# Gate and up projections on Trainium2: one of seven block products computed by seven products of quarter blocks

## The chip, the core and the metric

The kernel runs on one core of one Trainium2 chip. The metric is the device time of one execution in microseconds (us), the median over runs. A core has five engines with a queue of instructions each, worked in order: TensorE (PE in the profile, its weight loads PEld), VectorE (DVE), ScalarE (ACT), GpSimd (POOL) and SyncE (SP), which here issues DMAs. Operands lie in SBUF (128 partitions); TensorE writes its sums to PSUM, eight banks of 128 x 512 f32.

## What is computed

One post-norm encoder layer on 1024 tokens of width 1024: an input projection, bidirectional retention and windowed attention, an output projection, a layer norm that gives h, then a feed-forward part with a small gated embedding and a second layer norm. The part that matters here:

```python
g = jnp.einsum('bsd,df->bsf', h, w_ffn_gate)
up = jnp.einsum('bsd,df->bsf', h, w_ffn_up)
ffn = jnp.einsum('bsf,fd->bsd', jax.nn.silu(g) * up, w_ffn_down)
```

D = 1024, the hidden width is 2816 = 22 tiles of 128 ("f tiles").

## The kernel before

All large products are done in split precision: `split` (L70) puts a rounded high half on ScalarE (`hi`, L71) and the remainder on VectorE (`lo = raw - hi`, L72; both inputs in SBUF), and `mm3c` (L781) issues three matmuls, hi x hi, hi x lo and lo x hi, on L783, L784 and L785, into one PSUM bank. Each is 128 x 128 weights by 512 columns.

The gate and up stage takes two f tiles at a time (a `Pair`, 11 in all) and sees each pair as a product of 2 x 2 blocks: the left matrix is the weight (rows: the two f tiles; columns: the two halves of D), the right one h transposed (halves of D by halves of the tokens). It uses Winograd's form of Strassen's scheme: seven block products instead of eight, with sums of blocks before and after. Product 1 is a11 b11, product 2 a12 b21, products 5, 6, 7, 3 and 4 use sums. With M1 the first product: u2 = M1 + M6, u3 = u2 + M7 (the code adds M7 onto M6's bank and then M1), c11 = M1 + M2, c22 = u3 + M5, c21 = u3 + M4, c12 = u2 + M5 + M3. Products that share a sum accumulate in one bank: 1 and 2 in bank X, 6, 7 and 4 in Y, 5 and 3 in Z. Before a later product is added onto a bank, the value that it holds must have been read.

The right operands (h and its sums, `RIGHT`, L1160) are split once and stay in SBUF. The work is a list of units (`gunits`, L1290): one product p for m = 0 (gate) or m = 1 (up), 12 matmuls each; below "unit p/m". The order in a pair is 1, 6, 5, 2, 7, 4, 3 (pair 0: 1, 2, 6, 5, 7, 4, 3). A unit has three parts:

- `prep`: the weights are loaded by SP into `raw` and `ln` (`load`, L1176; at unit 1/m of the pair); the split of the unit's left operand into an operand slot, in turn from four `w` and four `u` tiles (L1197); behind unit 1/m GpSimd makes four block sums of weights (`s_sums`, L1183; L1187, L1188, L1190, L1191).
- `mm`: the matmuls (L1201).
- `post` (L1223): reads of the bank. `add` (L1231) is a VectorE addition of a bank and an SBUF tile (L1232); the copy of product 1 is on ScalarE (L1238). `finish` (L1211) applies Silu to the gate on ScalarE (L1215) and multiplies it with up on GpSimd (L1217). `asum` (L1219) makes sums of finished blocks for the down projection on GpSimd (L1221). Results go to DRAM (`ad`) by SP, two units later.

The order of the work is written out by hand: every engine executes its instructions in the order in which the program issues them. The loop at L1616 issues for each unit k its matmuls, its `post`, and then `ahead(2, k + 1 + min(8, 4 + k))` (L1583), which issues preparations up to eight units ahead; then stores that are due:

```python
for k in range(NG):
    gunits[k][1]()
    gunits[k][2]()
    ahead(2, k + 1 + min(8, 4 + k))
    while stores and stores[0][0] <= k:
        stores.pop(0)[1]()
```

Evicted blocks lie in `ev` tiles from a ring of eight (`pair_tile`, L1164); a pair takes seven. Each pair takes three of four bank tags in turn, two banks each (L1205). After this stage the down projection runs with its own lists (`d_units`, `d_step`).

Of the kernel before, what the change touches and what calls it, by code (L numbers as in the profile page):

```python
# [9 lines left out]
F32 = mybir.dt.float32  # L10
F32R = mybir.dt.float32r
AF = mybir.ActivationFunctionType
ALU = mybir.AluOpType
# [3 lines left out]
P = 128  # L17
# [4 lines left out]
HF = 512  # L22
# [20 lines left out]
def layer(tc, xT, xn, w_first, w_mt, w_rv, w_out, w_pg, w_pe, pT, w_gu, w_dn,  # L43
          consts, dec_b, dec_c, sink, gng, lnp, out):
    nc = tc.nc
    act, dve, pool, pe, sp = nc.scalar, nc.vector, nc.gpsimd, nc.tensor, nc.sync
# [8 lines left out]
    wp = cstack.enter_context(tc.tile_pool(name="wp", bufs=4))  # L55
# [14 lines left out]
    def split(raw, hi, lo):  # L70
        act.activation(hi, raw, AF.Copy)  # L71
        dve.tensor_tensor(lo, raw, hi.bitcast(F32), ALU.subtract)  # L72
# [77 lines left out]
    with tc.manual_schedule(engines={mybir.EngineType.DVE, mybir.EngineType.SP}):  # L150
        for kt in range(KT):
# [26 lines left out]
            w = wf[kt % 2]  # L178
# [10 lines left out]
    cst = cp.tile([P, C_W], F32, name="cst")  # L189
# [530 lines left out]
    with tc.manual_schedule(engines={mybir.EngineType.PE}):  # L720
# [7 lines left out]
        a = Attention(0, ytile(1))  # L728
# [11 lines left out]
        Q, X = (lambda q: (r.scores, q)), (lambda q: (r.turn, q))  # L740
        Y, E = (lambda q: (r.out, q)), (lambda q: (r.evict, q))
# [3 lines left out]
        for i in range(1, NPAIR):  # L745
# [26 lines left out]
    def ct(shape, tag, bufs=None, dt=F32):  # L772
        return cpool.tile(list(shape), dt, tag=tag, bufs=bufs, name=nm(tag))
# [7 lines left out]
    def mm3c(o, lh, ll, rh, rl, start, stop):  # L781

        pe.matmul(o, lh, rh, start=start, stop=False, skip_group_check=True)  # L783
        pe.matmul(o, lh, rl, start=False, stop=False, skip_group_check=True)  # L784
        pe.matmul(o, ll, rh, start=False, stop=stop, skip_group_check=True)  # L785
# [169 lines left out]
    c11 = [r[:, i * HF:(i + 1) * HF] for r in (rawt(2 * HF), rawt(2 * HF)) for i in range(2)]  # L955
# [5 lines left out]
    Z = four("b")  # L961
# [9 lines left out]
    X = four("a")  # L971
# [121 lines left out]
    X = four("a")  # L1093
# [25 lines left out]
    for k in range(4):  # L1119
        c = slice(k * P, (k + 1) * P)  # L1120
# [11 lines left out]
    Z = four("b")  # L1132
# [28 lines left out]
    sarena = arena8  # L1161
    ptags = ("mm", "s", "t", "o")

    def pair_tile():  # L1164
        return a_tile([P, 2, HF], "ev")

    stores = []

    class Pair:
# [23 lines left out]
        def prep(self, p, m, k):  # L1193
            src = {1: lambda: self.raw[m, 0, 0], 2: lambda: self.raw[m, 0, 1], 4: lambda: self.raw[m, 1, 1],
                   5: lambda: self.s[m][1], 6: lambda: self.s[m][0], 7: lambda: self.s[m][2],
                   3: lambda: self.s[m][3]}[p]()
            t = wp.tile([P, 2, HF], F32R, tag="w", bufs=4, name=nm("w")) if k % 2 == 0 else ct([P, 2, HF], "u", 4, F32R)  # L1197
            split(src, t[:, 0, :], t[:, 1, :])
            self.ops[p, m] = t

        def mm(self, p, m):  # L1201
            g = {1: 0, 2: 0, 6: 1, 7: 1, 4: 1, 5: 2, 3: 2}[p]
            first = p in (1, 6, 5)
            if first:
                self.bank[g, m] = bank(ptags[(3 * self.n + g) % 4])  # L1205
            b, w, r = self.bank[g, m], self.ops[p, m], RIGHT[p]
            for kt in range(4):
                c = slice(kt * P, (kt + 1) * P)
                mm3c(b, w[:, 0, c], w[:, 1, c], r[:, 0, kt, :], r[:, 1, kt, :], first and kt == 0, kt == 3)

        def finish(self, name, m):  # L1211

# [10 lines left out]
        def post(self, p, m, k):  # L1223
            ev, X, Y, Z = self.ev, self.bank.get((0, m)), self.bank.get((1, m)), self.bank.get((2, m))

            def get(name):
                if m == 0:
                    ev[name] = pair_tile()
                return ev[name][:, m, :]

            def add(name, left, right):  # L1231
                dve.tensor_tensor(get(name), ev[left][:, m, :], right, ALU.add)  # L1232

            a = lambda name: ev[name][:, 1, :]
            s = lambda name: ev[name][:, 0, :]
            wait = 2 if self.n < NP - 1 else 8
            if p == 1:
                act.activation(get("s1"), X, AF.Copy)  # L1238
            elif p == 6:
                add("u2", "s1", Y)  # L1240
            elif p == 2:
                c = get("c11")
                if m == 0:
                    act.activation(c, X, AF.Silu)
                else:
                    dve.tensor_tensor(c, ev["c11"][:, 0, :], X, ALU.mult)
            elif p == 7:
                add("u3", "s1", Y)
                add("c22", "u3", Z)
                self.finish("c22", m)  # L1250
            elif p == 4:
                add("c21", "s1", Y)
                self.finish("c21", m)
                if m:
                    self.asum("c21", a("c21"), a("c11"), ALU.subtract)
                    stores.append((k + wait, lambda: sp.dma_start(ad[self.n, 2, :, 0, :], s("c21"))))
                    self.asum("c11", s("c21"), a("c22"), ALU.subtract)
                    stores.append((k + wait, lambda: sp.dma_start(ad[self.n, 0], ev["c11"])))
                    self.asum("c22", a("c22"), a("c21"), ALU.subtract)
                    stores.append((k + wait, lambda: sp.dma_start(ad[self.n, 3], ev["c22"])))  # L1260
            elif p == 3:
                add("c12", "u2", Z)
                self.finish("c12", m)
                if m:
                    self.asum("c12", a("c12"), s("c11"), ALU.add)
                    stores.append((k + wait, lambda: sp.dma_start(ad[self.n, 1], ev["c12"])))

    NP = NHID // 2
    gunits = []
    pairs2 = [Pair(n) for n in range(NP)]  # L1270

    def g_unit(n, p, m, k):
        pr = pairs2[n]

        def prep():
            if p == 1 and n:
                pr.load(m)
            pr.prep(p, m, k)
            if p == 1:
                if n:  # L1280
                    pr.s_sums(m)
                else:
                    pr.s_sums(m, (0,))
                    if m:
                        pr.s_sums(0, (1,))
                        pr.s_sums(1, (1,))

        return prep, lambda: pr.mm(p, m), lambda: pr.post(p, m, k)
# [323 lines left out]

    ET = mybir.EngineType
    with tc.manual_schedule(engines={ET.PE, ET.DVE, ET.Activation, ET.Pool, ET.SP}):
        ahead(2, 4)
        for k in range(NG):  # L1616
            gunits[k][1]()
            gunits[k][2]()
            ahead(2, k + 1 + min(8, 4 + k))
            while stores and stores[0][0] <= k:  # L1620
                stores.pop(0)[1]()
            j = k + 1 - NG
            if j == -6:
                arenas_a()
                op_arena(ct([P, 4, 2, HF], "h0a", dt=F32R))
                op_arena(big16((P, 4, 2, HF)))
                op_arena(big16((P, 4, 2, HF)))
                arena("chain", ct([P, 8, HF], "h0b"), 8)
            if j == -4:
                op_arena(big16((P, 4, 2, HF)))  # L1630
                arena("b", big.tile([P, 8, HF], F32, tag="H", bufs=4, name=nm("H")), 8)
            if j >= -6:
                ahead(0, j + 7)
            if j >= -4:
                ahead(1, j + 5)
        arena("chain", ct([P, 8, HF], "h2"), 8)
        op_arena(ct([P, 4, 2, HF], "h3", dt=F32R), 4)
        rings["op"] += [ct([P, 2, HF], "u", 4, F32R) for _ in range(2)]
        for k in range(ND):
            d_step(k)  # L1640
# [85 lines left out]
```

## Time and profile before

| | us |
|---|---|
| median of 3 runs | 1181.1 (1179.52 to 1181.5) |
| the profiled execution | 1180.62 |
| its span, first to last instruction | 1178.8 |
| mean granted TensorE clock | 0.997 |
| gate and up stage on TensorE | 540 to 960 |
| GpSimd's block sums (L1187, L1188, L1190, L1191), 88 in all | 131.4 busy |

The profile's page gives busy time by engine, a picture of the span in 40 slices, the chain of work that ended last, and groups of instructions by line. Rows of the timeline read: start, duration (both us), engine, line, operation, output <- inputs, shape, count, and in brackets how long the engine sat idle before and what released it. A matmul's record (0.39 us for 512 columns) overlaps the next one's; the step between two starts is what one costs. In rows of stretches the columns are: stretch, length, busy us and number of instructions of PE, PEld, DVE, ACT and POOL, granted clock, share of the DMA engines, GB/s. In rows of waits: who <- on whom: us in total, times, longest.

### The profile page before, as it was taken

The page shows a single profiled execution, that of the slowest core. Times are in us where ns is not written, and L with a number is a line of the kernel's source. Part 1 is how long each engine was busy: PE and PEld are TensorE (multiplying, and loading weights), DVE is VectorE, ACT ScalarE, POOL GpSimd, SP SyncE. Part 2 cuts the span into 40 slices and gives each one's busy share as a digit, 9 for nine tenths or more (in the row PEclk, how much of TensorE's full clock was granted, in tenths as well). Part 3 has the DMA queues.
Part 4 walks back from the last instruction along what each step waited for, and adds up shares of the span by engine and source line. Part 5 has one row for each costly group of instructions (what it writes and reads, how often), then busy time and mean ns, then how long its engine had stood idle before and what let it go on. Part 6 is the DMA issues. An engine that isn't in the chain of part 4 may idle for free.

```text
span 1178.8 us, 17058 instructions
## 1 busy us (share of the span) xinstructions
PE 1167.3 (99%) x6068; PEld 968.4 (82%) x6068; DVE 767.3 (65%) x1310; ACT 534.4 (45%) x1049; POOL 365.5 (31%) x346
## 2 busy tenths in 40 slices
PE   9999999999999999999999999999999999999996
PEld 7888888888888888888788888888888888888885
DVE  5566678776849688948655455545555465774777
ACT  5566348777756265214332333323333325563463
POOL 2001010202010020004765647464655341134242
PEclk9999999999999999999999999999999999999998
DMA  6345656545346955665323331233213179999977
GB/s 253 107 148 215 241 182 240 188 152 205 123 151 240 361 186 195 242 221 176 124 76 120 134 110 70 90 134 135 77 63 129 72 221 323 354 270 229 258 164 208
DMA packets 80661, 211.71 MB, mean 180 GB/s; under 512 B 9536, under 2 KB 14784, under 8 KB 80576
## 3 DMA queue, kind: packets, MB, share of 16 engines
q1 hardware_dynamic: 71936, 193.84, 46.2%
q0 software_dynamic: 8640, 16.78, 8.0%
q8 instruction: 48, 0.79, 0.3%
q14 instruction: 37, 0.30, 0.1%
HBM read 139.29 MB, written 62.13 MB: 171 GB/s over the span
## 4 chain that ended last, share of the span: by engine, by line
PE 94%; DVE 3%; ACT 1%; issue 1%; DMA 1%; DVEq 0%; SPq 0%; ACTq 0%
PE bmm L77 6%; PE bs L785 6%; PE bs L783 6%; PE bs L784 6%; PE bmm L79 6%; PE bmm L78 6%; PE bt L783 5%; PE bt L785 5%; PE bt L784 5%; PE bmm L785 5%; PE bmm L783 5%; PE bmm L784 5%; PE bo L785 5%; PE bo L783 5%; PE bo L784 5%; PE bo L565 2%
## 5 line engine op out<-in xcount | busy, mean ns | idle before, releaser
L77 PE MATMUL bmm<-H,w 128*128 128x512 f32 x240 | 97.2, 405 | 0.2 <-ACT H L71 0.2
L79 PE MATMUL bmm<-H,w 128*128 128x512 f32 x240 | 94.1, 392 | 0.0
L78 PE MATMUL bmm<-H,w 128*128 128x512 f32 x240 | 94.0, 392 | 0.0
L1187 POOL TENSOR_TENSOR H<-ln 128x512 f32<-128x512 f32 x22 | 28.9, 1312 | 180.2 <-ACT w L71 96.1
L1217 POOL TENSOR_TENSOR ev<-ev 128x512 f32<-128x512 f32 x33 | 55.4, 1679 | 90.6 <-DVE ev L1232 63.6
L72 DVE TENSOR_TENSOR w<-H,w 128x512 fp32r<-128x512 f32 x44 | 41.6, 945 | 62.7 <-ACT w L71 62.7
L72 DVE TENSOR_TENSOR w<-raw,w 128x512 fp32r<-128x512 f32 x56 | 46.3, 832 | 47.3 <-ACT w L71 47.1
L526 POOL COPY sc<-skb 128x1 f32<-128x1 f32 x64 | 14.8, 240 | 182.5 <-PE bt L553 162.5
L1215 ACT ACTIVATE ev<-ev 128x512 f32<-128x512 f32 x33 | 20.9, 632 | 103.5 <-DVE ev L1232 103.5
L1221 POOL TENSOR_TENSOR ev<-ev,ev 128x512 f32<-128x512 f32 x44 | 62.7, 1436 | 2.6
L72 DVE TENSOR_TENSOR u<-H,u 128x512 fp32r<-128x512 f32 x47 | 38.0, 809 | 36.6 <-ACT u L71 36.2
L77 PEld LDWEIGHTS bmm<-H,w 128*128 128x128 f32 x240 | 45.1, 188 | 10.3 <-ACT H L71 1.1
L79 PEld LDWEIGHTS bmm<-H,w 128*128 128x128 f32 x240 | 45.0, 188 | 10.0
L78 PEld LDWEIGHTS bmm<-H,w 128*128 128x128 f32 x240 | 45.2, 188 | 7.8
L71 ACT ACTIVATE u<-H 128x512 fp32r<-128x512 f32 x47 | 29.6, 630 | 43.3 <-POOL H L1188 11.1
L535 ACT ACTIVATE sc<-sc,st 128x385 f32<-128x385 f32 (+1 forms) x64 | 37.2, 584 | 17.1 <-DVE st L533 17.0
L71 ACT ACTIVATE w<-raw 128x512 fp32r<-128x512 f32 x56 | 34.5, 623 | 18.8 <-PE bmm L79 6.9
L531 DVE CUSTOM_DVE_ANT_0 sc<-cst,bs,skb 128x384 f32<-128x384 f32 (+1 forms) x64 | 34.9, 577 | 9.2 <-PE bs L530 7.9
L493 POOL TENSOR_TENSOR sm<-sm,cst 128x8 f32<-128x8 f32 x8 | 13.8, 1727 | 79.9 <-DVE sm L492 79.9
L894 POOL TENSOR_TENSOR stt<-stt,cst 128x1 f32<-128x1 f32 x8 | 12.2, 1520 | 83.8 <-DVE stt L893 83.8
L1191 POOL TENSOR_TENSOR H<-raw,H 128x512 f32<-128x512 f32 x22 | 37.3, 1697 | 0.0
L71 ACT ACTIVATE w<-H 128x512 fp32r<-128x512 f32 x44 | 27.3, 621 | 21.0 <-PE bs L785 6.3
(813 smaller groups left out, 3756.2 us busy)
## 6 DMA issues: line engine op xcount, KB each, us to landing
ad<-ev SPq DMA_DIRECT2D x33, 512.0 KB, 2.6
pgd<-pro SPq DMA_DIRECT2D x28, 512.0 KB, 3.0
raw<-in_w_gu SPq DMA_DIRECT2D x22, 512.0 KB, 4.5
ln<-in_w_gu SPq DMA_DIRECT2D x22, 512.0 KB, 3.6
raw<-ad SPq DMA_DIRECT2D x40, 256.0 KB, 5.5
ln<-ad SPq DMA_DIRECT2D x37, 256.0 KB, 6.4
H<-in_w_dn SPq DMA_DIRECT2D x33, 256.0 KB, 6.6
wod<-aq SPq DMA_DIRECT2D x15, 512.0 KB, 2.7
```

What stands on the lines that cost most here:

```text
L71: act.activation(hi, raw, AF.Copy)
L72: dve.tensor_tensor(lo, raw, hi.bitcast(F32), ALU.subtract)
L77: pe.matmul(o, lh, rh, start=start, stop=False)
L78: pe.matmul(o, lh, rl, start=False, stop=False)
L79: recent[0] = pe.matmul(o, ll, rh, start=False, stop=stop).ins.name
L535: act.activation(sc[g][:, :nk + 1], sc[g][:, :nk + 1], AF.Exp, bias=st_[:, 1, j, g:g + 1], accum_out=st_[:, 2, j, g:g + 1])
L783: pe.matmul(o, lh, rh, start=start, stop=False, skip_group_check=True)
L784: pe.matmul(o, lh, rl, start=False, stop=False, skip_group_check=True)
L785: pe.matmul(o, ll, rh, start=False, stop=stop, skip_group_check=True)
L1191: pool.tensor_tensor(s[3], a(0, 1), s[0], ALU.subtract)
L1217: pool.tensor_tensor(c[:, 1, :], c[:, 0, :], c[:, 1, :], ALU.mult)
L1221: pool.tensor_tensor(self.ev[dst][:, 0, :], left, right, op)
```

## The change

From pair 1 on, product 1 (units 1/0 and 1/1) is not done as 24 matmuls of 512 columns. Its left block (two f tiles by half of D) and its right block (half of D by 512 tokens) are cut again into 2 x 2, and seven products of quarter blocks are done by the same scheme: 7 x 2 x 3 = 42 matmuls of 256 columns, in three fine parts with products 1, 6, 5, then 7, 2, then 4, 3. They use two banks, and their reads build M1 in the tile `s1` by narrow (256) copies and additions.

The left quarter sums are made per pair by VectorE (`prep_fine`: four subtractions or additions of 256), followed by five splits into four operand slots, and then GpSimd's eight block sums for the pair. The right quarter sums are made once, in pair 0, behind units 2, 4, 6 and 8 (`fine_right`), with the constants' tile as scratch. Product 2 no longer accumulates on product 1's bank: c11 is formed by a VectorE addition, then Silu in place, and for m = 1 a VectorE product. The order of a pair is now fine 0, 5/0, fine 1, 5/1, fine 2, 6, 2, 7, 4, 3. c22, c21 and c12 are summed in place over u3, s1 and u2, so a pair needs four `ev` tiles from a ring of seven. Operand slots are eight tiles handed out in turn and given back when the unit's matmuls are issued; a unit is prepared only if enough are free (fine part 0 needs four, parts 1 and 2 none, others one). The weights of pair n+1 are loaded behind the preparations of products 2 and 4 of pair n.

```diff
+    FINE = ((1, 6, 5), (7, 2), (4, 3))
+        def prep_fine(self):
+            x, y = (self.raw[m, 0, 0] for m in range(2))
+            b = [y[:, :Q], y[:, Q:]]
+            t = [take_op() for _ in range(4)]
+            for o, l, r_, op in ((fsum[0], *b, add), (fsum[1], x[:, :Q], b[0], sub),
+                                 (fsum[2], fsum[0], x[:, :Q], sub), (fsum[3], x[:, Q:], fsum[2], sub)):
+                dve.tensor_tensor(o, l, r_, op)
+            split(x, t[0][:, 0, :], t[0][:, 1, :])
+            split(fsum2, t[2][:, 0, :], t[2][:, 1, :])
+            split(fsum[2], t[3][:, 0, :Q], t[3][:, 1, :Q])
+            split(b[1], t[1][:, 0, :Q], t[1][:, 1, :Q])
+            split(fsum[3], t[1][:, 0, Q:], t[1][:, 1, Q:])
...
+        def post_fine(self, part):
...
+            if part == 0:
+                act.activation(c21, bx, AF.Copy)
+                dve.tensor_tensor(c12, c21, by, ALU.add)
+            elif part == 1:
+                dve.tensor_tensor(c21, c21, by, ALU.add)
+                dve.tensor_tensor(c22, c21, bz, ALU.add)
+                act.activation(c11, bx, AF.Copy)
+            else:
+                dve.tensor_tensor(c21, c21, bw, ALU.add)
+                dve.tensor_tensor(c12, c12, bz, ALU.add)
...
+        return prep, lambda: pr.mm_fine(part), lambda: pr.post_fine(part), (4, 0, 0)[part]
     for n in range(NP):
-        for p in (1, 6, 5, 2, 7, 4, 3) if n else (1, 2, 6, 5, 7, 4, 3):
+        for p in (5, 6, 2, 7, 4, 3) if n else (1, 2, 6, 5, 7, 4, 3):
             for m in range(2):
+                if n and p == 5:
+                    gunits.append(f_unit(n, m))
                 gunits.append(g_unit(n, p, m, len(gunits)))
+            if n and p == 5:
+                gunits.append(f_unit(n, 2))
...
-        while done[what] < min(upto, len(units)):
+        while done[what] < min(upto, len(units)) and (what < 2 or units[done[2]][3] <= len(oslots)):
...
             gunits[k][2]()
+            if 2 <= k <= 8 and k % 2 == 0:
+                fine.pop(0)()
             ahead(2, k + 1 + min(8, 4 + k))
```

More of the change, by code (lines that the diff above doesn't have):

```diff
@@ L1162, in layer, with take_op, free_op, fine_right @@
     ptags = ("mm", "s", "t", "o")
-    def pair_tile():
-        return a_tile([P, 2, HF], "ev")
+    Q = HF // 2
+    FINE = ((1, 6, 5), (7, 2), (4, 3))
+    evs, nev = [], [0]
+    oslots = []
+    fright, fsum = {}, []
+    def pair_tile():
+        nev[0] += 1
+        return evs[(nev[0] - 1) % len(evs)]
+    def take_op():
+        return oslots.pop(0)
+    def free_op(t):
+        oslots.append(t)
+    def fine_right(R):
+        x = cst[:, 0:HF].rearrange("p (k c) -> p k c", k=2)
+        def blk(i, j, part):
+            return R[:, part, 2 * i:2 * i + 2, j * Q:(j + 1) * Q]
+        def both(left, right):
+            dve.tensor_tensor(x, blk(*left, 0).bitcast(F32), blk(*right, 0).bitcast(F32), ALU.subtract)
+            dve.tensor_tensor(x, x, blk(*left, 1).bitcast(F32), ALU.add)
+            dve.tensor_tensor(x, x, blk(*right, 1).bitcast(F32), ALU.subtract)
+        def less(left):
+            dve.tensor_tensor(x, blk(*left, 0).bitcast(F32), x, ALU.subtract)
+            dve.tensor_tensor(x, x, blk(*left, 1).bitcast(F32), ALU.add)
+        for q, (i, j) in {1: (0, 0), 2: (1, 0), 3: (1, 1)}.items():
+            fright[q] = blk(i, j, 0), blk(i, j, 1)
+        spare_ = a_tile([P, 2, 2, Q], "fine", dt=F32R)
+        fright[7] = spare_[:, 0], spare_[:, 1]
+        fright[5] = tuple(ct([P, 2, Q], "sg", 2, F32R) for _ in range(2))
+        fright[6] = tuple(ct([P, 2, Q], "p", 2, F32R) for _ in range(2))
+        fright[4] = blk(0, 1, 0), blk(0, 1, 1)
+        return [lambda: (both((1, 1), (0, 1)), split(x, *fright[7])), lambda: (both((0, 1), (0, 0)), split(x, *fright[5])),
+                lambda: (less((1, 1)), split(x, *fright[6])), lambda: (less((1, 0)), split(x, *fright[4]))]
     stores = []
@@ L1196, in prep @@
                    3: lambda: self.s[m][3]}[p]()
-            t = wp.tile([P, 2, HF], F32R, tag="w", bufs=4, name=nm("w")) if k % 2 == 0 else ct([P, 2, HF], "u", 4, F32R)
+            t = self.ops[p, m] = take_op()
             split(src, t[:, 0, :], t[:, 1, :])
-            self.ops[p, m] = t
+        def prep_fine(self):
+            x, y = (self.raw[m, 0, 0] for m in range(2))
+            b = [y[:, :Q], y[:, Q:]]
+            f = self.fine = {}
+            t = [take_op() for _ in range(4)]
+            sub, add = ALU.subtract, ALU.add
+            for o, l, r_, op in ((fsum[0], *b, add), (fsum[1], x[:, :Q], b[0], sub),
[6 more added lines that the diff above has]
+            split(fsum[3], t[1][:, 0, Q:], t[1][:, 1, Q:])
+            for q, (i, j) in {1: (0, 0), 2: (0, 1), 5: (2, 0), 7: (2, 1), 6: (3, 0), 4: (1, 0), 3: (1, 1)}.items():
+                f[q] = t[i], slice(j * Q, (j + 1) * Q)
@@ new lines, in mm_fine @@
+        def mm_fine(self, part):
+            if part == 0:
+                self.fb = [bank(ptags[3 * self.n % 4]) for _ in range(2)]
+            for q in FINE[part]:
+                t, c0 = self.fine[q]
+                i, j = {1: (0, 0), 2: (0, 0), 6: (0, 1), 7: (0, 1), 5: (1, 0), 3: (1, 0), 4: (1, 1)}[q]
+                o = self.fb[i][:, j * Q:(j + 1) * Q]
+                hi, lo = fright[q]
+                for kt in range(2):
+                    c = slice(c0.start + kt * P, c0.start + (kt + 1) * P)
+                    mm3c(o, t[:, 0, c], t[:, 1, c], hi[:, kt, :], lo[:, kt, :], q in (1, 5) and kt == 0, kt == 1)
+            for i in {0: (3,), 1: (0, 2), 2: (1,)}[part]:
+                free_op(self.fine[{3: 6, 0: 1, 2: 5, 1: 4}[i]][0])
@@ new lines, in post_fine @@
+        def post_fine(self, part):
+            if part == 0:
+                self.ev["s1"] = pair_tile()
+            o = self.ev["s1"]
+            (c11, c12), (c21, c22) = ([o[:, m, j * Q:(j + 1) * Q] for j in range(2)] for m in range(2))
+            (bx, by), (bz, bw) = ([b[:, j * Q:(j + 1) * Q] for j in range(2)] for b in self.fb)
+            if part == 0:
+                act.activation(c21, bx, AF.Copy)
[7 more added lines that the diff above has]
+                dve.tensor_tensor(c12, c12, bz, ALU.add)
@@ L1201, in mm @@
         def mm(self, p, m):
             g = {1: 0, 2: 0, 6: 1, 7: 1, 4: 1, 5: 2, 3: 2}[p]
-            first = p in (1, 6, 5)
+            first = p in (1, 6, 5) or p == 2 and self.n > 0
             if first:
@@ L1209, in mm @@
                 mm3c(b, w[:, 0, c], w[:, 1, c], r[:, 0, kt, :], r[:, 1, kt, :], first and kt == 0, kt == 3)
+            free_op(w)
         def finish(self, name, m):
@@ L1229, in get, with add @@
                 return ev[name][:, m, :]
-            def add(name, left, right):
-                dve.tensor_tensor(get(name), ev[left][:, m, :], right, ALU.add)
+            def add(name, left, right, over=False):
+                if over and m == 0:
+                    ev[name] = ev[left]
+                dve.tensor_tensor(ev[name][:, m, :] if over else get(name), ev[left][:, m, :], right, ALU.add)
             a = lambda name: ev[name][:, 1, :]
@@ L1240, in post @@
                 add("u2", "s1", Y)
+            elif p == 2 and self.n:
+                add("c11", "s1", X)
+                if m == 0:
+                    act.activation(s("c11"), s("c11"), AF.Silu)
+                else:
+                    dve.tensor_tensor(a("c11"), s("c11"), a("c11"), ALU.mult)
             elif p == 2:
@@ L1248, in post @@
                 add("u3", "s1", Y)
-                add("c22", "u3", Z)
+                add("c22", "u3", Z, True)
                 self.finish("c22", m)
             elif p == 4:
-                add("c21", "s1", Y)
+                add("c21", "s1", Y, True)
                 self.finish("c21", m)
@@ L1261, in post @@
             elif p == 3:
-                add("c12", "u2", Z)
+                add("c12", "u2", Z, True)
                 self.finish("c12", m)
@@ L1614, in layer @@
     with tc.manual_schedule(engines={ET.PE, ET.DVE, ET.Activation, ET.Pool, ET.SP}):
+        for _ in range(4):
+            oslots.append(wp.tile([P, 2, HF], F32R, tag="w", bufs=4, name=nm("w")))
+            oslots.append(ct([P, 2, HF], "u", 4, F32R))
+        fine = fine_right(RIGHT[1])
+        evs.extend(a_tile([P, 2, HF], "ev") for _ in range(7))
+        fsum2 = cst[:, 0:HF]
+        fsum.extend([cst[:, 0:Q], cst[:, Q:2 * Q], cst[:, 2 * Q:3 * Q], ct([P, Q], "fs", 1)])
         ahead(2, 4)
```

22 lines of the change are left out of this document (13 added, 9 removed).

## The prediction, made before the changed kernel was run

> **What bounds the kernel now.** I read the page's busy shares first, then the chain of work that ended last, then TensorE's waits inside the gate and up stage, then one pair of f tiles as a stretch of its own.
>
> ```profile
> PE 1167.3 (99%) x6068; PEld 968.4 (82%) x6068; DVE 767.3 (65%) x1310; ACT 534.4 (45%) x1049; POOL 365.5 (31%) x346
> ...
> PE 94%; DVE 3%; ACT 1%; issue 1%; DMA 1%; DVEq 0%; SPq 0%; ACTq 0%
> ```
> ```profile
> PE bs L783 <- DVE ev L1232: 0.7, 1, 0.7
> ```
> ```profile
> 696.60:734.63 38.03, 38.03 (x170) 31.48 (x169) 19.86 (x25) 11.88 (x20) 22.26 (x16) 1.00 0.29 104
> ```
>
> TensorE is busy 99% of the span and is 94% of the chain. In the stage the change touches it waited once, 0.7 us. A steady pair takes 38.03 us: 168 matmuls of 512 columns, 0.2264 us each, so a unit of 12 takes 2.72 us. The clock granted is 1.00. VectorE is busy 19.9 us of the 38 and GpSimd 22.3: both look half empty. So time falls only if TensorE gets less to do, and rises as soon as an operand or a bank comes later than TensorE reaches it.
>
> **What TensorE saves.** In pairs 1 to 10, product 1 (24 matmuls of 512 columns) becomes 42 of 256. The trace has 256-column matmuls of the same type, four in a row:
>
> ```profile
> 54.22 0.28 PE L529 MATMUL bs<-k,aq 128*128 128x256 f32 x1
> 54.33 0.28 PE L530 MATMUL bs<-kz,aq 128*128 128x256 f32 x1
> 54.45 0.28 PE L529 MATMUL bs<-k,aq 128*128 128x256 f32 x1
> 54.57 0.28 PE L530 MATMUL bs<-kz,aq 128*128 128x256 f32 x1
> 54.69 0.40 PE L77 MATMUL bmm<-H,w 128*128 128x512 f32 x1
> ```
>
> From 54.22 to 54.69 they step by 0.1175 us; bounds are half a wide one (0.113) and the 0.12 of the widest step. 24 x 0.2264 = 5.43 us becomes 42 x 0.1175 = 4.94: 0.50 us a pair (0.4 to 0.7), 5.0 us in ten. That is the whole possible gain, 0.4%.
>
> **What it costs beside TensorE.** Before, a pair gives VectorE 14 low-half subtractions of 512. After: 14 of 512 and 3 of 256, four block sums of 256, five narrow bank additions and two more wide operations. What matters is when. Eight operand slots exist; the preparation of fine part 0 takes four at once, so it is issued only after unit 7/1 (product 7, tile 1). Ahead of TensorE are then 4/0, 4/1, 3/0, 3/1: 10.87 us, where before eight units (21.7 us) were ready. In that moment VectorE gets nine operations with all operands in SBUF (four sums, low halves of 512, 512, 256, 256, 256) and GpSimd gets, right behind its product for c22, the eight sums of the next pair. The trace shows such operations meet:
>
> ```profile
> 549.33 1.73 POOL L1191 TENSOR_TENSOR H<-raw,H 128x512 f32<-128x512 f32 x1
> 551.02 1.74 POOL L1190 TENSOR_TENSOR H<-raw,ln 128x512 f32<-128x512 f32 x1
> 552.73 1.74 POOL L1191 TENSOR_TENSOR H<-raw,H 128x512 f32<-128x512 f32 x1
> ...
> 563.13 1.28 POOL L1188 TENSOR_TENSOR H<-H,raw 128x512 f32<-128x512 f32 x1
> 564.37 1.29 POOL L1190 TENSOR_TENSOR H<-raw,ln 128x512 f32<-128x512 f32 x1
> ...
> 717.36 1.73 POOL L1191 TENSOR_TENSOR H<-raw,H 128x512 f32<-128x512 f32 x1
> ```
> ```profile
> 549.84 1.77 DVE L72 TENSOR_TENSOR w<-H,w 128x512 fp32r<-128x512 f32 x1
> 551.53 1.78 DVE L72 TENSOR_TENSOR u<-H,u 128x512 fp32r<-128x512 f32 x1
> 553.23 1.78 DVE L72 TENSOR_TENSOR w<-H,w 128x512 fp32r<-128x512 f32 x1
> 554.94 0.68 DVE L72 TENSOR_TENSOR u<-H,u 128x512 fp32r<-128x512 f32 x1
> 555.54 0.68 DVE L72 TENSOR_TENSOR w<-H,w 128x512 fp32r<-128x512 f32 x1
> ...
> 718.54 0.69 DVE L1232 TENSOR_TENSOR ev<-ev,bs 128x512 f32<-128x512 f32 x1 [0.59 <-PE bs L785]
> 719.26 0.69 DVE L1232 TENSOR_TENSOR ev<-ev,bmm 128x512 f32<-128x512 f32 x1
> ```
> ```profile
> L1026 DVE TENSOR_TENSOR H<-H,h 128x1024 f32<-128x1024 f32 x2 | 2.5, 1225 | 0.1
> ```
>
> While GpSimd works, VectorE's SBUF subtractions end about 0.55 us after each GpSimd operation, one for one, every 1.70 us; once GpSimd is done they step by 0.60. GpSimd alone steps by 1.24 to 1.25. So the pair of operations costs 1.25 + 0.45, and VectorE waits out a whole GpSimd operation each time. An addition with one input in PSUM (718.54) runs its 0.69 us beside GpSimd. The width of 256 is not in the trace with two SBUF inputs. Bounds: 1.25 (it adds nothing) and 1.70 (like 512). A step from 512 to 1024 columns adds 1225 - 690 = 535 ns, so 256 takes some 0.27 off the 0.45: 1.44 us, the value I take.
>
> The Trainium skill, "SBUF — State Buffer", Who interferes with whom, says that VectorE with two SBUF inputs and GpSimd exclude each other and that the winner holds the ports for the whole instruction. By whole instructions a round would be 1.29 + 0.69 = 1.98, and eight rounds some 2 us more; the 1.70 between these rows says a little of each overlaps, and I keep 1.70.
>
> The other steps of the chain:
>
> ```profile
> 734.60 0.39 PE L783 MATMUL bo<-h0a,u 128*128 128x512 f32 x1
> 734.80 0.60 ACT L1238 ACTIVATE ev<-bo 128x512 f32<-128x512 f32 x1 [2.03 <-PE bo L785]
> ```
> ```profile
> 720.03 0.63 ACT L1215 ACTIVATE ev<-ev 128x512 f32<-128x512 f32 x1 [3.64 <-DVE ev L1232]
> 720.57 0.61 ACT L71 ACTIVATE w<-H 128x512 fp32r<-128x512 f32 x1
> ```
> ```profile
> 570.46 0.67 DVE L1232 TENSOR_TENSOR ev<-ev,bs 128x512 f32<-128x512 f32 x1
> 571.28 0.47 PE L783 MATMUL bs<-h,u 128*128 128x512 f32 x1 [0.72 <-DVE ev L1232]
> ```
>
> A bank is read 0.2 us after the next unit's first matmul (734.60); ScalarE starts 0.08 us after VectorE's end at 719.95 and steps by 0.54; TensorE follows VectorE's end by 0.15.
>
> Clock of one pair, T = 0 when unit 7/1 ends on TensorE, orders of the queues as the changed program has them:
>
> 1. VectorE: the two additions of 7/1 at 0.2 and 0.8; first sum at 1.4, before GpSimd can start (1.6). The other eight operations wait out one GpSimd operation each: 6 x 1.44 + 2 x 1.70 = 12.0. From 1.7 the last low half is done at **13.8** (0.1 for a dependent GpSimd sum). Fine part 0 (10.87 to 12.97) finds its operands: they come first.
> 2. Behind that on VectorE stands the c21 addition of unit 4/0 (to 14.5); ScalarE's Silu waits for it (14.6), and behind the Silu, in order, the high half of 5/0 (15.15 to 15.8). TensorE wants it at 12.97 and gets it at 15.9: **2.9 us idle**. 5/0 runs to 18.6.
> 3. Fine part 1 adds product 7 onto the bank half that VectorE must first read (u2 = M1 + M6, the narrow c12 addition of part 0). Before that read the queue holds: low 5/0 (its high half is there at 15.8, done 16.5), c21 addition (17.2), low 5/1 (17.8), c12 addition (18.4), low 6/0, which needs a high half queued behind the Silu of c12 (19.65) and then meets GpSimd's sum (done 20.55), c12 addition (21.2), low 6/1 behind another GpSimd sum (22.25), then the narrow read (0.42): 22.7. TensorE starts part 1 at 22.8 instead of 18.6: **4.2 us idle**.
> 4. Then 12 narrow, 5/1, 12 narrow, six units: 1.41 + 2.72 + 1.41 + 16.3 = 21.85, all with operands in time. The pair lasts 22.8 + 21.85 = 44.65 us against 38.03: **+6.6**, the saving of 0.5 included.
>
> Ten pairs: +66. Pair 1 adds something: fourteen operations for the fixed operands go into VectorE's queue during pair 0.
>
> ```profile
> 560.95 0.68 DVE L72 TENSOR_TENSOR w<-raw,w 128x512 fp32r<-128x512 f32 x1
> 565.03 1.18 DVE L72 TENSOR_TENSOR u<-raw,u 128x512 fp32r<-128x512 f32 x1 [3.41 <-ACT u L71]
> ```
>
> VectorE ran dry at 561.6 there; 14 x 0.6 = 8.4 us more and the four bank additions it must do by then put it at about 571.8 where 569.2 is wanted, so pair 1's clock is some 2.6 us late (0 to 4). Sum: 1180.6 (the profiled execution's time, 0.5 below the median shown) + 66 + 2.6 = **1249 us**.
>
> Costs I put at nothing. The weights of pair n+1 are now loaded during pair n:
>
> ```profile
> POOL H L1187 <- DMA ln<-in_w_gu: 76.9, 9, 8.8
> ...
> ln<-in_w_gu SPq DMA_DIRECT2D x22, 512.0 KB, 3.6
> ```
>
> GpSimd waited for these loads in nine pairs; now they are issued over 10 us ahead and take 3.6, so the sums meet VectorE at once. On SP the loads stand behind stores that wait for GpSimd's c22 sum (T + 23.5); that leaves 10 us, and if it went, the next T would slip by the excess. Sums in place need seven ev tiles; a slot is reused two pairs later or, for c21, about one, some 10 us after its store: hidden.
>
> **The rivals.** (a) *The waits do not chain; it gets faster.* The lost time decides from one point: part 1 is on time if the last low half is done by T + 8 rather than 13.8, that is if VectorE waits under 0.36 us per operation ((8 - 5.1) / 8) instead of 1.1. With none it is done at 5.1 (1.4, four sums and three narrow halves of 0.35, two wide ones of 0.6), no stall is left, and the time is 1180.6 - 5 = 1176 us. For it: GpSimd and VectorE are half empty over the pair. Against: the three rows of 1.77 us, and that both are released by the same two additions. 13%. (b) *Half of it*: GpSimd starts its sums later or gaps in its chain let VectorE through twice; done at 9 to 11, only part 1 waits, 1.4 to 3.5 us: 1190 to 1225. 20%. (c) *Idle costs more than its length.*
>
> ```profile
> 1.31 3.59 PE L142 MATMUL bo<-sq 128*128 128x512 bf16 x8 [1.31 <-POOL sq L139]
> ```
>
> Eight matmuls of 512 columns took 3.59 us at the start, 0.45 each, twice the later step. If a gap of 4.2 us brought that back for the 4.1 us of work after it, each pair would lose 2 to 4 us more: 1269 to 1289. The granted clock stays at 1.00 in the stretch above, where no gap exceeds 1 us, so the trace cannot decide. The Trainium skill, "TensorE: Matmul & The Clock Gate", HAM oscillation, has the clock halve after an idle window of about 3.4 us; by that rule a gap of 4.2 would do so in some pairs only. 9%. (d) *Little or nothing*, the stall just eating the 0.5 a pair: 1179 to 1183. 4%. That the narrow products are not executed is excluded: TensorE's list grows by 18 matmuls in each of ten pairs.
>
> **How the numbers follow.** The forecast has 54%. Its own range comes from the narrow round: 1.25 to 1.70 moves the last low half, and with it part 1, by -1.1 to +1.6 us a pair, 1237 to 1265. For 8 in 10 I add nearly all of (b), from 1192, and (c) to 1280: 0.54 + 0.19 + 0.06 = 0.79; (a), (d) and the far ends stay out. A measurement tells 0.2% from no change: faster 0.13, same 0.04, slower 0.83.
>
> **What would show it.** In the changed profile a steady pair should last 43.5 to 46 us, with two TensorE gaps: one at 5/0 released by ScalarE's high half (2 to 4 us), one at the first narrow matmul of part 1 released by VectorE (3 to 5.5 us). Narrow matmuls should step by 0.117. The block sums should last 1.2 to 1.5 us each instead of some 0.4. If they last 0.4, or the pair lasts 37.5, the contention step is wrong; if the gaps are there but matmuls behind them step by 0.45, it is (c); if TensorE waits at fine part 0, the operand order is wrong.

## The result, and the profile after

| | before | after |
|---|---|---|
| median, us (six runs each, side by side) | 1180.35 (1179.48 to 1181.5) | 1275.11 (1272.72 to 1278.9) |
| span of the profiled execution, us | 1178.8 | 1271.1 |
| mean granted TensorE clock | 0.997 | 0.967 |
| a steady pair, us | 38.03 | 44.87 to 47.68 |

The changed kernel takes 1.0806 times as long (95%: 1.0784 to 1.0827). The forecast was 1249, so the direction is right and 26 us are missing from it.

The page of the changed kernel: busy times, and the granted clock in 40 slices.

```profile
PE 1201.4 (95%) x6248; PEld 996.3 (78%) x6248; DVE 905.9 (71%) x1464; ACT 539.6 (42%) x1083; POOL 369.4 (29%) x346
...
PEclk9999999999999999998988998998998999999999
```

The same row of the clock before:

```profile
PEclk9999999999999999999999999999999999999998
```

TensorE's list grew by the 180 matmuls that were added, and it is busy 34 us longer although the narrow matmuls take the place of more work. The clock has six notches between the 19th and the 31st slice, all in the gate and up stage; before, no notch is there. The largest groups among TensorE's waits, one of each kind:

```profile
PE bo L783 <- DVE ev L1281: 7.9, 3, 3.7
...
PE bt L783 <- ACT u L71: 5.3, 2, 2.6
```

The other large groups are of these two kinds, both forecast: L71 is ScalarE's high half (for unit 5/0), L1281 the narrow bank read that fine part 1 waits for. Where before the stage had one wait of 0.7 us, each pair now has two. One pair on TensorE; unit 7/1 ended at 758.65, the T = 0 of the prediction:

```profile
758.65 0.39 PE L783 MATMUL bs<-h,u 128*128 128x512 f32 x1
...
769.53 0.28 PE L783 MATMUL bo<-h0a,u 128*128 128x256 f32 x1
...
774.49 0.50 PE L783 MATMUL bs<-H,u 128*128 128x512 f32 x1 [2.65 <-ACT u L71]
...
781.48 0.58 PE L783 MATMUL bo<-fine,w 128*128 128x256 f32 x1 [3.70 <-DVE ev L1281]
781.86 0.42 PE L784 MATMUL bo<-fine,w 128*128 128x256 f32 x1
...
784.21 0.63 PE L783 MATMUL bs<-H,u 128*128 128x512 f32 x1
784.63 0.63 PE L784 MATMUL bs<-H,u 128*128 128x512 f32 x1
...
788.24 0.28 PE L783 MATMUL bo<-h0a,w 128*128 128x256 f32 x1
...
789.67 0.40 PE L783 MATMUL bt<-H,w 128*128 128x512 f32 x1
```

Fine part 0 comes on time. Unit 5/0 starts at T + 15.84 (forecast 15.9), part 1 at T + 22.83 (forecast 22.8). What VectorE did in those microseconds:

```profile
759.65 0.69 DVE L1324 TENSOR_TENSOR ev<-ev,bmm 128x512 f32<-128x512 f32 x1
760.25 0.42 DVE L1248 TENSOR_TENSOR cst<-raw 128x256 f32<-128x256 f32 x1
760.59 1.52 DVE L1248 TENSOR_TENSOR cst<-raw,raw 128x256 f32<-128x256 f32 x1
762.03 1.51 DVE L1248 TENSOR_TENSOR cst<-cst,raw 128x256 f32<-128x256 f32 x1
763.58 1.40 DVE L1248 TENSOR_TENSOR fs<-raw,cst 128x256 f32<-128x256 f32 x1
764.90 1.78 DVE L72 TENSOR_TENSOR u<-raw,u 128x512 fp32r<-128x512 f32 x1
766.60 3.21 DVE L72 TENSOR_TENSOR w<-cst,w 128x512 fp32r<-128x512 f32 x2
769.73 1.51 DVE L72 TENSOR_TENSOR w<-raw,w 128x256 fp32r<-128x256 f32 x1
771.17 1.50 DVE L72 TENSOR_TENSOR w<-fs,w 128x256 fp32r<-128x256 f32 x1
772.58 0.67 DVE L1324 TENSOR_TENSOR ev<-ev,bs 128x512 f32<-128x512 f32 x1
774.47 0.69 DVE L72 TENSOR_TENSOR u<-H,u 128x512 fp32r<-128x512 f32 x1 [1.22 <-ACT u L71]
...
775.68 0.68 DVE L72 TENSOR_TENSOR u<-H,u 128x512 fp32r<-128x512 f32 x1
...
778.18 1.23 DVE L72 TENSOR_TENSOR w<-H,w 128x512 fp32r<-128x512 f32 x1 [1.22 <-ACT w L71]
...
779.93 1.16 DVE L72 TENSOR_TENSOR u<-H,u 128x512 fp32r<-128x512 f32 x1
781.02 0.41 DVE L1281 TENSOR_TENSOR ev<-ev,bo 128x256 f32<-128x256 f32 x1
```

GpSimd at the start of this, with its product for c22 and the first block sum:

```profile
760.48 1.34 POOL L1307 TENSOR_TENSOR ev<-ev 128x512 f32<-128x512 f32 x1 [19.73 <-DVE ev L1324]
761.78 1.48 POOL L1226 TENSOR_TENSOR H<-ln 128x512 f32<-128x512 f32 x1
```

The first narrow sum, begun ahead of GpSimd's start at 760.48, takes 0.42 us; the same work beside GpSimd takes 1.4 to 1.5. The last low half ends at T + 14.0 (forecast 13.8). The rows from 774.47 on are the queue of step 3: the low halves of 5/0, 5/1, 6/0 and 6/1, and then, without a pause, the narrow read at 781.02. ScalarE starts the Silu that stood in front of 5/0's high half when the addition of 772.58 is done, having been idle 7.86 us behind VectorE:

```profile
773.29 0.63 ACT L1305 ACTIVATE ev<-ev 128x512 f32<-128x512 f32 x1 [7.86 <-DVE ev L1324]
773.83 1.14 ACT L71 ACTIVATE u<-H 128x512 fp32r<-128x512 f32 x2
```

What the forecast lacks is behind the second gap. The narrow matmuls there step by 0.21 us instead of 0.12 (eleven steps from 781.86 to 784.21), the wide ones of 5/1 by 0.42 to 0.43 instead of 0.23. Stretches of that pair and of the pair before (columns as in the section on the profile before):

```profile
729.62:774.49 44.87, 40.74 (x186) 33.61 (x186) 32.96 (x40) 12.15 (x24) 22.65 (x15) 0.93 0.26 88
774.49:821.86 47.37, 41.02 (x186) 34.11 (x187) 33.22 (x40) 12.16 (x24) 22.62 (x15) 0.92 0.25 84
781.48:786.60 5.12, 5.12 (x18) 4.64 (x19) 4.57 (x6) 1.42 (x3) 4.04 (x3) 0.50 0.95 318
```

For 5.12 us behind the gap the granted clock is 0.50. Measured from one 5/0 to the next, six of nine pairs last 47.24 to 47.68, three 44.87 to 44.91. In the short ones the clock falls in the first gap, and what that costs only shortens the second, since VectorE sets the start of part 1. In the longest, which begins at 961.63, it falls in both gaps, 2.65 and 2.67 us.

### The profile page after: what moved, and what is told of

Its sections match the earlier page's. It is cut to its first block, busy times and chain, and to the rows that moved or that the text cites. A ratio compares the mean times of both kernels' runs of the same rounds, so it can differ in the third digit from the quotient of the medians.

```text
span 1271.1 us, 17584 instructions
## 1 busy us (share of the span) xinstructions
PE 1201.4 (95%) x6248; PEld 996.3 (78%) x6248; DVE 905.9 (71%) x1464; ACT 539.6 (42%) x1083; POOL 369.4 (29%) x346
## 5 line engine op out<-in xcount | busy, mean ns | idle before, releaser
L1307 POOL TENSOR_TENSOR ev<-ev 128x512 f32<-128x512 f32 x33 | 51.6, 1565 | 262.7 <-DVE ev L1324 217.8
L72 DVE TENSOR_TENSOR w<-raw,w 128x512 fp32r<-128x512 f32 (+1 forms) x56 | 57.5, 1033 | 17.2 <-ACT w L71 16.7
L1311 POOL TENSOR_TENSOR ev<-ev,ev 128x512 f32<-128x512 f32 x44 | 68.0, 1554 | 2.6
L1226 POOL TENSOR_TENSOR H<-ln 128x512 f32<-128x512 f32 x22 | 35.4, 1608 | 96.5 <-DMA ln<-in_w_gu 96.5
L72 DVE TENSOR_TENSOR w<-H,w 128x512 fp32r<-128x512 f32 x45 | 38.3, 858 | 20.6 <-ACT w L71 20.6
L71 ACT ACTIVATE w<-raw 128x512 fp32r<-128x512 f32 (+1 forms) x56 | 33.8, 612 | 17.4 <-PE bo L79 7.9
L71 ACT ACTIVATE u<-H 128x512 fp32r<-128x512 f32 x46 | 28.3, 621 | 29.7 <-PE bt L784 6.3
L1324 DVE TENSOR_TENSOR ev<-ev,bo 128x512 f32<-128x512 f32 x32 | 21.9, 684 | 26.7 <-PE bo L785 26.5
L1324 DVE TENSOR_TENSOR ev<-ev,bt 128x512 f32<-128x512 f32 x34 | 23.2, 683 | 23.3 <-PE bt L785 23.1
L72 DVE TENSOR_TENSOR u<-raw,u 128x512 fp32r<-128x512 f32 (+1 forms) x26 | 36.8, 1415 | 4.2 <-ACT u L71 4.2
L493 POOL TENSOR_TENSOR sm<-sm,cst 128x8 f32<-128x8 f32 x8 | 13.8, 1728 | 79.7 <-DVE sm L492 79.7
```

Source lines behind the costliest of these rows:

```text
L1307: pool.tensor_tensor(c[:, 1, :], c[:, 0, :], c[:, 1, :], ALU.mult)
L1311: pool.tensor_tensor(self.ev[dst][:, 0, :], left, right, op)
L1324: dve.tensor_tensor(ev[name][:, m, :] if over else get(name), ev[left][:, m, :], right, ALU.add)
```

## The experiments

Each edit is against the changed kernel. Unit "3/1" is product 3, tile 1; "pair 0/1" means the passage from pair 0 to pair 1.

**e1: GpSimd's eight block sums issued earlier**, with the preparation of unit 3/1 of the pair before, so that they no longer run beside VectorE's narrow sums.

```diff
@@ g_unit, preparation
+            if n + 1 < NP and (p, m) == (3, 1):
+                for i in range(2):
+                    pairs2[n + 1].s_sums(i)
@@ f_unit, preparation of part 0
-                for m in range(2):
-                    pr.s_sums(m)
```

> GpSimd's eight block sums of pair n+1 are issued behind the preparation of unit 3/1 of pair n, some eight units earlier, instead of behind the preparation of fine part 0; nothing else moves. If the lost time is VectorE waiting out GpSimd's sums (the forecast's mechanism): no gap at unit 5/0, at most 0.5 us at fine part 1, VectorE's four block sums of 256 at about 0.4 us each, a pair near 144 x 0.2264 + 42 x 0.12 = 37.6 us, time 1176 to 1184 us (1180 less 4, plus up to 3 for pair 0's own waits). If the lead of four units is too short by itself (slots, VectorE's own work): both gaps stay within 1 us of 2.65 and 3.7, time above 1240 us.

Measured: 1189.99 us (1189.66 to 1191.6), ratio 1.0083 (1.0063 to 1.0103). A steady pair, TensorE's waits in the stage, and the narrow sums:

```profile
633.78:671.52 37.74, 37.74 (x188) 32.06 (x186) 25.69 (x40) 12.07 (x23) 21.84 (x16) 1.00 0.30 105
```
```profile
PE bs L783 <- DVE ev L1324: 7.0, 3, 4.4
PE bo L783 <- DVE ev L1281: 0.9, 1, 0.9
```
```profile
L1248 DVE TENSOR_TENSOR cst<-raw,raw x10: 1518/1519/1537, 582.5 to 921.9; 128x256 f32<-128x256 f32 x10
L1248 DVE TENSOR_TENSOR cst<-cst,raw x10: 410/410/412, 584.0 to 923.3; 128x256 f32<-128x256 f32 x10
```

Both stalls are gone from pairs 2 to 10 and with them 85 of the 95 us; the total is still 6 us above the expected 1176 to 1184. All gaps left, 7.9 us, lie in pair 0/1, where the fixed right quarter sums put fourteen operations into VectorE's queue and now meet the early block sums (e6 and e8 test this); the granted clock there is 0.94. Of the narrow sums only the second still takes 1.52 us, because it meets GpSimd's product for c22.

**e2: GpSimd only writes.** Same place and order, but 0.5 is written into the eight tiles instead of their sums, so the block sums of pairs 1 to 10 are left out.

```diff
-                    pr.s_sums(m)
+                    pr.s[m] = [sarena[:, 4 * m + i, :] for i in range(4)]
+                    for i in (1, 0, 2, 3):
+                        pool.memset(pr.s[m][i], 0.5)
```

> At the place of the eight block sums GpSimd writes a constant into the same eight tiles, eight memsets of 128x512; the sums of the weights for pairs 1 to 10 are left out. GpSimd is then busy at the same moment but reads nothing. If VectorE's wait is for GpSimd's reads of SBUF: VectorE's block sums and low halves run at their own 0.4 and 0.69 us, gap at 5/0 under 0.5 us, time 1176 to 1190 us. If any GpSimd instruction holds VectorE up for its whole length: about 0.9 us a memset (two of 64x1024 took 947 ns each in the trace of before), so VectorE's chain shrinks from 12 to about 8 us, the first gap goes and the second falls to 1 to 2 us, time 1195 to 1215 us.

Measured: 1184.53 us, one run. The narrow sum and the writes:

```profile
L1248 DVE TENSOR_TENSOR cst<-cst,raw x10: 410/411/414, 578.5 to 917.9; 128x256 f32<-128x256 f32 x10
...
L1394 POOL MEMSET H<- x80: 518/521/532, 578.3 to 920.9; 128x512 f32 x80
```

The writes took 0.52 us and not the 0.9 expected, so GpSimd was also busy for a shorter time: 3.8 us in all. But the narrow sum that ran right beside the first of them took 0.41 us where beside a sum it takes 1.51. TensorE's gaps in the stage, some 5 us in all, lie in pairs 0 and 1; from pair 2 on there is none. It is reading beside reading that costs. This agrees with the Trainium skill, "SBUF — State Buffer", Who interferes with whom, by which a VectorE operation with two SBUF inputs contends with a GpSimd instruction that reads SBUF and not with one that only writes it.

**e3: filler matmuls in the gaps, into the fourth bank** (10 ahead of 5/0, 14 ahead of part 1; nobody reads their results), to keep the clock up.

```diff
+                pe.matmul(self.idle[0], r[:, 0, 2, 0:P], r[:, 0, 2, :], start=True, stop=True, ...)
...
+                self.idle = [bank(ptags[(3 * self.n + 3) % 4]) for _ in range(2)]
```

> The changed kernel with extra matmuls of 512 columns into an idle bank, whose result nobody reads: 10 (2.3 us) before unit 5/0 and 14 (3.2 us) before fine part 1 of every pair, a little less than the gaps there. They add 240 matmuls and move no other engine. If idle time lets the clock fall (steps of 0.21 us for narrow matmuls and longer ones for wide ones behind a gap): the steps are 0.12 everywhere, the granted clock is back near 1.00, every pair lasts 44.9 us instead of 44.9 to 47.7, time 1252 to 1260 us, so work that is added saves 13 to 20 us. If the clock has another cause: no less than 1272 us, more if the fill is longer than a gap.

Measured: 1318.44 us (1316.87 to 1319.63), ratio 1.1172 (1.1146 to 1.1198). The fillers themselves waited:

```profile
PE bs L1261 <- DVE ev L1335: 15.5, 3, 5.2
```

The fourth bank still held products 5 and 3 of the pair before, and their last read stands in the same late queue of VectorE. So the edit made a third stall of 5.2 us a pair and says nothing about the clock.

**e4: fewer units prepared ahead**, five from unit 9 on, so that 6/0 and 6/1 do not stand ahead of the narrow read.

```diff
-            ahead(2, k + 1 + min(8, 4 + k))
+            ahead(2, k + 1 + (min(8, 4 + k) if k < 9 else 5))
```

> Preparations run at most five units ahead from pair 0's unit 4/0 minus one on, not eight, so those of 6/0 and 6/1 are issued behind the bank reads of fine part 0 instead of ahead of them; fine part 0 and 5/0 are prepared where they were. If the second gap is the narrow bank read queued on VectorE behind 6/0 and 6/1 (step 3 of the forecast): the gap before fine part 1 falls from 3.7 to 1 to 2 us, the one at 5/0 stays 2.65, a pair is some 2.3 us shorter, and with the clock falling less often the time is 1230 to 1255 us. If the second gap is GpSimd or the bank itself: it stays, 1270 us or more.

Measured: 1246.67 us (1245.03 to 1248.53), ratio 1.0561 (1.0538 to 1.0584).

```profile
765.90 0.50 PE L783 MATMUL bs<-H,u 128*128 128x512 f32 x1 [3.12 <-ACT u L71]
...
771.48 0.39 PE L783 MATMUL bo<-fine,w 128*128 128x256 f32 x1 [1.05 <-DVE ev L1281]
```

The second gap fell from 3.70 to about 1 us, the first rose from 2.65 to 3.12. Steady pairs last 43.94 to 44.12. But most of that fall is not the order of the queue. In this pair T is 749.58, so 5/0 starts at T + 16.32, 0.48 later than in the changed kernel, and it runs 1.24 longer, because the clock fell behind the first gap (its matmuls step by 0.43 from 767.67 on). Part 1 starts at T + 21.90, only 0.93 earlier, and steady pairs are shorter than the short ones of 44.87 to 44.91 by about as much, not by the 2.3 expected. So the order ahead of the narrow read has a share in when part 1 starts, and a smaller one than the gap suggests; the first gap has another cause.

**e5: the same fillers, into product 6's bank**, which unit 6/0 overwrites later.

```diff
+                pe.matmul(self.bank[1, 0], r[:, 0, 2, 0:P], r[:, 0, 2, :], start=True, stop=True, ...)
...
+                    self.bank[1, m] = bank(ptags[(3 * self.n + 1) % 4])
```

> The fill of e3_warm once more, 10 extra matmuls before unit 5/0 and 14 before fine part 1 of every pair, now into the bank that product 6 takes next, which has been read long before; their result is overwritten. If idle time lets the clock fall: narrow steps of 0.12 and wide ones of 0.23 everywhere, granted clock 0.99 or more, every pair 44.9 us, time 1250 to 1260 us, 13 to 20 us below the changed kernel's although 240 matmuls are added. If the clock has another cause, or a fill outlasts its gap: 1272 us or more.

Measured: 1256.28 us (1255.69 to 1257.56), ratio 1.0646 (1.063 to 1.0663), span 1253.6, clock 0.998. The gap ahead of part 1, and the pair:

```profile
770.29 0.50 PE L783 MATMUL bs<-H,u 128*128 128x512 f32 x1 [0.38 <-ACT u L71]
...
773.45 3.34 PE L1261 MATMUL bt<-h0a 128*128 128x512 f32 x14
777.33 0.39 PE L783 MATMUL bo<-fine,w 128*128 128x256 f32 x1 [0.54 <-DVE ev L1293]
```
```profile
770.29:815.26 44.97, 44.05 (x211) 36.33 (x211) 33.07 (x40) 12.10 (x24) 22.76 (x15) 1.00 0.25 88
```

240 matmuls more, and the span is 17.5 us shorter: part 1 starts as late as before, but at clock 1.00, and all pairs now last 44.95 to 44.97. This is the clock's share by itself.

**e6: e1, with quarter products only from pair 2**, the right quarter sums behind units 16 to 19.

```diff
-            if 2 <= k <= 8 and k % 2 == 0:
+            if 16 <= k <= 19:
...
-                    gunits.append(f_unit(n, m))
+                    gunits.append(f_unit(n, m) if n > 1 else g_unit(n, 1, m, len(gunits)))
```

> As e1_early_sums, but with the quarter products from pair 2 on: pair 1 does product 1 whole and makes its sums at that unit as before the change, and the right quarter sums are made during pair 1 (behind units 16 to 19), not during pair 0. If the 8 us of gaps in e1's pairs 0 and 1 come from those fourteen operations in VectorE's fullest stretch: they go, leaving at most 1 us as in the kernel before; nine pairs save 0.29 us each (37.74 against 38.03 in e1), time 1176.5 to 1179.5 us, just below the kernel before. If they come from something else in the change (weight loads, slots, the separate bank of product 2): gaps of 3 us or more stay in pairs 0 and 1, 1181 us or more.

Measured: 1182.8 us (1182.09 to 1184.55), ratio 1.002 (1.001 to 1.003). One gap is left, at 7/0 of pair 1:

```profile
PE bt L783 <- DVE ev L1324: 3.1, 1, 3.1
```

The right sums met GpSimd's early sums for pair 2, so the same meeting had only been moved. This missed the expected range by 3 us, about the length of the gap.

**e7: everything but the quarter products**: product 1 whole in all pairs, new buffers, loads, in-place sums and slots kept.

```diff
-                    gunits.append(f_unit(n, m))
+                    gunits.append(g_unit(n, 1, m, len(gunits)))
...
-            if 2 <= k <= 8 and k % 2 == 0:
-                fine.pop(0)()
```

> All of the change except the quarter products: sums in place, seven ev tiles, slots given back, weights loaded a pair ahead, product 2 in a bank of its own, the order with products 1 and 5 interleaved; product 1 stays 24 wide matmuls in all pairs, its right quarter sums are not made. If these parts cost nothing (the forecast): 1179 to 1182 us, pairs of 38.03 us, no gap above 1 us. If one of them carries part of the 95 us: 1190 us or more, with gaps in steady pairs.

Measured: 1181.06 us (1180.03 to 1182.83), ratio 1.0005 (0.9996 to 1.0014); TensorE has no gap in the stage, and a steady pair is the one of before:

```profile
696.60:734.63 38.03, 38.03 (x169) 31.33 (x168) 22.41 (x28) 11.79 (x20) 22.45 (x16) 1.00 0.31 104
```

**e8: e6 with the right sums spread out**, behind units 12, 14, 16 and 17.

```diff
-            if 2 <= k <= 8 and k % 2 == 0:
+            if k in (12, 14, 16, 17):
```

> e6_from_pair2 with the right quarter sums made behind units 12, 14, 16 and 17, where GpSimd is idle or short of work, not behind 16 to 19, where they run into GpSimd's early sums for pair 2. If e6's one gap (3.1 us at unit 7/0 of pair 1) is these fourteen operations meeting those sums: it goes or falls below 1 us, and the time is some 2.5 to 3 us below e6, 1178 to 1181 us: level with the kernel before or up to 2 us under it, since all that nine pairs save is 2.6 us. If the gap comes from the load on VectorE alone: it moves to another unit and the time stays at 1182 to 1184 us.

Measured: 1178.94 us (1178.44 to 1181.01, eleven runs) against 1180.22, ratio 0.9994 (0.9984 to 1.0003). e6's gap at 7/0 is gone, but one of 1.7 us is left, at pair 2's part 1. There three of the four narrow sums still take 1.50 to 1.51 us, from 607.42 on: GpSimd's early sums for that pair end only at 610.08.

```profile
661.17:698.91 37.74, 37.74 (x188) 32.06 (x187) 27.49 (x40) 12.06 (x23) 21.68 (x16) 1.00 0.31 105
```

Cleared of its stalls, the change is level with the kernel before within what can be measured. Nine pairs that save 0.29 us each give 2.6 us, 0.2%, less the gap of 1.7.

## Why the prediction was right in its mechanism and short in its sum

The 92.3 us between the two spans (1178.8 and 1271.1) come apart like this:

| term | forecast | measured | from |
|---|---|---|---|
| two stalls, ten pairs | +71 | +72.3 | e5's pair 44.97 less e1's 37.74, times ten |
| narrow matmuls, ten pairs | -5.0 | -2.9 | e1's 37.74 against 38.03, times ten |
| passage of pair 0/1 | +2.6 | +4.7 | e5's gaps in the passage, 4.9, and 0.5 by which pair 1's first gap is longer than later ones, against 0.7 before |
| clock behind the gaps | 0 | +17.5 | 1271.1 less e5's 1253.6 |
| sum | +68.6 | +91.6 | 92.3 measured |

*What bounds the kernel* (TensorE, and nothing else in this stage) held: e7 changes buffers, loads and the order of sums and is level with before.

*Step 1* held. Eight operations waited out one GpSimd operation each, and the last low half came 0.2 us from the forecast. The chosen 1.44 us for a round of 256 is borne out: the starts of the narrow operations in the rows above step by 1.3 to 1.55. That the meeting is the cause is shown twice: e1 moves GpSimd's sums away and e2 takes their reads away, and in both the steady pairs run without a stall. By the rule of the Trainium skill, "SBUF — State Buffer", SBUF: two separate sides, that whichever of the two starts first keeps the ports for its whole instruction, a narrow round would be 1.29 + 0.42 = 1.71; the narrow steps of this case are shorter, and the measurement decides.

*Step 2* held (gap 2.65 against 2.9), *step 3* too (3.70 against 4.2; its start is exact, and 5/0 ended a little later than put). The rows of VectorE follow step 3 one by one: low 5/0 from T + 15.8, low 6/1 done at T + 22.4, the read done at T + 22.8. The order alone does not make the gap, though: e4 changes it and part 1 comes only 0.93 us earlier, while e1 keeps it and has no second gap from pair 2 on. VectorE's queue is late as a whole, because of step 1.

*What TensorE saves* was mis-sized: 0.29 us a pair and not 0.50. The step of 0.1175 came from four matmuls in a row; in runs of twelve it is 0.119, as from 788.24 to 789.67 above, and in the runs of 18 it reaches 0.12, the upper bound that the prediction had named. The first wide matmuls behind them step by 0.23 to 0.24.

*The sum* failed at one step: it counted idle time at its own length. Rival (c) priced the lost clock at 2 to 4 us a pair and gave it 9%; it came, in six of nine pairs at some 2.5 us, with its sign: wide matmuls at a step of 0.43. The prediction treated (c) as an alternative to the forecast, though the forecast's own gap of 4.2 us was all that (c) needed. Added as a term, by (c)'s own figures, it would have given 1269 or more. So 1275 lies outside the forecast's own range of 1237 to 1265, and inside 1192 to 1280 only because (c) had been added there with 0.06.

The Trainium skill, "TensorE: Matmul & The Clock Gate", HAM oscillation, has the clock halve after an idle window of about 3.4 us. Here all five gaps of 3.70 brought the clock down, and not some only as the prediction took from that rule; but the clock did not wait for 3.4 us of idle time, and four of the nine gaps of 2.65 us at unit 5/0 brought it down as well. Which ones can be read from this trace. In every trace in which the clock changes it does so only at steps of a grid of 3.41 us; cut there, every stretch has one clock. TensorE's idle time in a stretch is its length less PE's busy time:

```profile
725.54:728.95 3.41, 1.43 (x12) 1.22 (x11) 2.84 (x3) 0.54 (x2) 3.36 (x3) 1.00 0.00 0
728.95:732.37 3.42, 2.75 (x7) 2.13 (x8) 2.49 (x4) 1.39 (x4) 1.35 (x1) 0.50 0.00 0
...
769.91:773.32 3.41, 1.94 (x17) 1.73 (x15) 3.35 (x3) 0.03 (x1) 3.41 (x3) 1.00 0.00 0
773.32:776.74 3.42, 2.25 (x9) 1.56 (x10) 2.27 (x4) 1.64 (x3) 1.31 (x2) 1.00 0.01 2
776.74:780.15 3.41, 1.04 (x5) 0.54 (x3) 2.19 (x4) 2.98 (x6) 3.25 (x3) 1.00 0.13 49
780.15:783.57 3.42, 2.09 (x10) 2.09 (x10) 3.42 (x4) 0.00 (x0) 3.42 (x3) 0.50 0.62 246
```

The gap ahead of 729.62 puts 1.98 us of idle time into one stretch, and the next has clock 0.50. The gap ahead of 774.49 is as long, but the grid splits it into 1.47 and 1.17, and the clock stays. The gap of 3.70 puts 2.37 us into one stretch, and from 780.15 on, before it is over, the clock is 0.50. In the gate and up stage of this run all 13 stretches at full clock with 1.89 us or more of idle time were followed by a slow one, and none with 1.84 or less. The other runs fit, except that one stretch of e4 with only 1.66 was followed by a slow one too. A gap of 2.15 us brought the clock down in e1, where it fell into one stretch, and one of the same length in e4, split into 1.16 and 0.98, did not. What decides, as far as these traces show, is how much of a gap falls into one stretch of the grid; no run moved a gap along the grid with nothing else changed.

*Pair 1's extra* was named with its cause and put 2 us too low.

Of the costs put at nothing, earlier loads, the ring of seven and in-place sums cost nothing: e7. The remark that GpSimd no longer waits for the loads, and so meets VectorE at once, is what step 1 rests on, and the rows of GpSimd bear it out: its first block sum follows its product for c22 without a wait.

## What to carry to other kernels

Before replacing long TensorE work by more vector work, draw the queues at the moment where operand slots come free, and look for two engines that are released by the same event and both read two SBUF operands: half-empty engines over a pair say nothing about that moment. A gap on TensorE of some 2 us or more is to be counted with the slow clock that may follow, here 2.3 to 2.7 us a pair, as a term of the sum and not as another case. And size the gain first: seven products of quarter blocks instead of eight were worth 0.29 us in 38 here, so the smallest stall eats it.

## What the runs showed of the hardware beyond that

- Behind a gap of 3.70 us the granted clock was 0.50 for 5.1 us, though TensorE was busy without a break; of nine gaps of 2.65 us at unit 5/0 four brought it down, by how much of a gap fell into one stretch of a grid of 3.41 us.
- Idle time filled with matmuls whose results nobody reads made the span 17.5 us shorter (e5), but only into a bank whose last read is early: in another bank the fillers waited 5.2 us a pair themselves (e3).
- GpSimd writing a constant to 128 x 512 f32 takes 0.52 us and leaves VectorE's two-input operations at 0.41 (e2); GpSimd adding two tiles of that size makes the same operations take 1.51.
